# Pairs of weight blocks packed column by column in turns in a two-block transformer kernel

## The chip, the cores and the metric

The kernel runs on one core of a Trainium2 chip. The metric is the device time of one execution in microseconds. Before the change it is 1784.51 us, the median of three runs (1778.77, 1784.51 and 1785.51).

## What is computed

Two transformer blocks of different make run one after the other on 256 positions of width 1024, each with two layers. Everything is float32. Per layer the work is dominated by products of the activations with weight matrices that are used once:

```
h = rmsnorm(x, g);  proj = h @ w_in[l]            # first block: 1024 x 7168
merged = gate0*(.. @ w_ret_out) + gate1*(.. @ w_sc_out) + gate2*(.. @ w_cf_out)
x = x + rmsnorm(merged @ w_o[l], g)
up = causal_dwconv(rmsnorm(x, g) @ w_up[l])       # 1024 x 5632
x = x + rmsnorm((silu(gate) * val) @ w_down[l], g)
...
z = rms(x, g) @ w_in_2[l]                         # second block: three attention-like branches
x = x + merged @ w_out_2[l]
x = x + (silu(g) * u) @ w_down_2[l]
```

Between them stand retention, short and long depthwise convolutions, an mLSTM, a top-k sparse attention and a differential attention, all small beside the weight products.

## The kernel before

All weights are packed on the host into one stream of chunks of 128 partitions by 1024 columns of float32. A chunk holds eight **blocks** of 128 x 128 (`CB = 8`, line 26). `plan()` (line 66) lists the jobs in the order in which the kernel takes them; `pack_weights` (line 127) cuts each job's weights into blocks in the order in which they are used, and puts block i at columns 128 (i mod 8) of chunk i // 8.

On the chip, `Weights.load_to` (line 302) loads chunks by SyncE's queue into four buffers `wraw`. `Weights.ensure` (line 311) splits each chunk into two float32r tiles: ScalarE writes the rounded part `whi` (line 326), VectorE the remainder `wlo` (the subtraction at line 328, recorded at line 417). `Weights.take` (line 336) hands out the next n blocks of a chunk as slices of `whi` and `wlo`; four chunks, listed by `whole_chunks`, are handed out unsplit as `wraw`.

`Gen.job` (line 492) does one job. Kind "B" takes one block at a time: the block is the stationary operand (128 x 128), the moving operand is one 128 x 256 slice of the activations, also split (`hh` and `hl`, `yh` and `yl`, `fh` and `fl`). Three products per block add into one PSUM accumulator `acc`: hi x hi, hi x lo and lo x hi (lines 515 to 518); `self.mm` records all of them at line 405. For an unsplit block there is one float32 product, which the trace shows as four passes. Kind "A" (line 531; the values of the attention branches) takes four blocks at once and uses them as a moving operand of 512 columns, with the activations as the stationary one. At fixed points of a job, `self.side()` lets the other tasks issue their instructions, so now and then products of theirs (into `sp` tiles) stand between those of the jobs.

Before the change, a block that is a stationary operand is 128 columns in a row: 512 bytes in each partition, at a step of 4 bytes.

Of the kernel before, what the change touches and what calls it, by code (L numbers as in the profile page):

```python
# [17 lines left out]
P = 128  # L18
# [108 lines left out]
def pack_weights(inputs):  # L127
    blocks = []
    cache = {}
    for arr, idx, kind, nk, cols in plan():  # L130
        key = (arr, idx)
        if key not in cache:
            cache[key] = np.asarray(inputs[arr])[idx]
        w = cache[key]
        if kind == "B":
            c = np.concatenate(cols)
            t = w[:, np.maximum(c, 0)]
            if (c < 0).any():
                t = np.where(c[None, :] < 0, np.zeros_like(t), t)
            n = len(cols)  # L140
            blocks.append(t.reshape(nk, P, n, P).transpose(0, 2, 1, 3).reshape(nk * n, P, P))
        else:
            t = w[:, cols].reshape(nk, P, 4, P).transpose(0, 2, 1, 3).reshape(nk * 4, P, P)
            blocks.append(t)
    n = sum(b.shape[0] for b in blocks)
    tot = -(-n // CB) * CB
    out = np.zeros((tot // CB, P, CB, P), np.float32)
    i = 0
    for b in blocks:
        for j in range(b.shape[0]):  # L150
            out[(i + j) // CB, :, (i + j) % CB, :] = b[j]
        i += b.shape[0]
    return out.reshape(tot // CB, P, CW)
# [129 lines left out]
class Weights:  # L283
# [52 lines left out]
    def take(self, n=1):  # L336
        c, b = divmod(self.cur, CB)
        assert b + n <= CB
        self.cur += n
        s = slice(b * P, (b + n) * P)  # L340
        return [y[:, s] for y in self.parts[c]]

# [1294 lines left out]
```

## Time and profile before

| | |
|---|---|
| median of three runs | 1784.51 us |
| the profiled execution, its own time | 1783.79 us |
| its span, first to last instruction | 1782.1 us |
| TensorE products (PE) | busy 1770.8 us (99%), 14462 |
| TensorE weight loads (PEld) | busy 1723.9 us (97%), 14462 |
| VectorE (DVE) | busy 1360.8 us (76%) |
| ScalarE (ACT) | busy 1110.6 us (62%) |
| GpSimd (POOL) | busy 69.7 us (4%) |
| read from HBM | 312.80 MB, 176 GB/s over the span |

PE and PEld are two rows of the same engine: a product (MATMUL) and the load of its stationary operand (LDWEIGHTS). Both are pipelined: each row lasts longer than the time from its start to the next one's start, so busy shares say little, and the rate is read from starts. The chain of waits follows the work back from the last instruction and merges neighbours on one engine and tile into pieces: a piece gives its start, its length and its number of instructions. [...]

### The profile page before, as it was taken

The page shows a single profiled execution, that of the slowest core. Times are in us where ns is not written, and L with a number is a line of the kernel's source. Part 1 is how long each engine was busy: PE and PEld are TensorE (multiplying, and loading weights), DVE is VectorE, ACT ScalarE, POOL GpSimd, SP SyncE. Part 2 cuts the span into 40 slices and gives each one's busy share as a digit, 9 for nine tenths or more (in the row PEclk, how much of TensorE's full clock was granted, in tenths as well). Part 3 has the DMA queues.
Part 4 walks back from the last instruction along what each step waited for, and adds up shares of the span by engine and source line. Part 5 has one row for each costly group of instructions (what it writes and reads, how often), then busy time and mean ns, then how long its engine had stood idle before and what let it go on. Part 6 is the DMA issues. An engine that isn't in the chain of part 4 may idle for free.

```text
span 1782.1 us, 35765 instructions
## 1 busy us (share of the span) xinstructions
PE 1770.8 (99%) x14462; PEld 1723.9 (97%) x14462; DVE 1360.8 (76%) x2082; ACT 1110.6 (62%) x1787; POOL 69.7 (4%) x144
## 2 busy tenths in 40 slices
PE   8999999999999999999999999999999999999999
PEld 8999999999999999999998999999999999999999
DVE  8998689866999779883988877855569887687553
ACT  7676568755666568764676666644457666655442
POOL 0000000000000000000022100000001210000000
PEclk9999999999999999999999999999999999999999
DMA  7655545555555545555555644555555664455553
GB/s 269 195 177 187 191 143 202 190 189 172 200 177 190 180 149 195 190 189 166 164 191 181 210 133 146 190 185 187 188 185 172 202 196 137 144 188 189 188 189 121
DMA packets 94648, 322.52 MB, mean 181 GB/s; under 512 B 12257, under 2 KB 16913, under 8 KB 94482
## 3 DMA queue, kind: packets, MB, share of 16 engines
q1 hardware_dynamic: 91010, 314.15, 53.1%
q0 software_dynamic: 3328, 6.09, 1.2%
q8 instruction: 113, 1.85, 0.4%
q14 instruction: 53, 0.43, 0.1%
q10 hardware_dynamic: 144, 0.00, 0.0%
HBM read 312.80 MB, written 1.10 MB: 176 GB/s over the span
## 4 chain that ended last, share of the span: by engine, by line
PE 97%; DVE 1%; DMA 1%; issue 1%; ACT 0%; POOL 0%; SPq 0%; DVEq 0%; ACTq 0%; POOLq 0%
PE acc L405 90%; PE sp L405 6%; PE sp L410 1%; DMA Wm<-rows 0%; DMA tmp<-dq 0%; DMA x<-x 0%; DVE sc L1169 0%; DVE x L417 0%; DVE m L1168 0%; DVE yw L422 0%; DVE wlo L417 0%; ACT sd L447 0%; DVE dq L417 0%; ACT whi L326 0%; DVE Wm L428 0%
## 5 line engine op out<-in xcount | busy, mean ns | idle before, releaser
L326 ACT ACTIVATE whi<-wraw 128x1024 fp32r<-128x1024 f32 (+1 forms) x575 | 606.5, 1057 | 529.6 <-PE acc L405 359.6
L417 DVE TENSOR_TENSOR wlo<-wraw,whi 128x1024 fp32r<-128x1024 f32 (+1 forms) x575 | 697.0, 1218 | 285.9 <-ACT whi L326 284.8
L405 PE MATMUL acc<-hh,whi 128*128 128x256 f32 x2832 | 791.4, 280 | 0.0
L405 PE MATMUL acc<-hl,whi 128*128 128x256 f32 x2832 | 791.0, 280 | 0.0
L405 PE MATMUL acc<-hh,wlo 128*128 128x256 f32 x2832 | 789.8, 280 | 0.0
L405 PEld LDWEIGHTS acc<-hh,whi 128*128 128x128 f32 x2832 | 534.0, 189 | 5.5 <-issue 3.7
L405 PEld LDWEIGHTS acc<-hh,wlo 128*128 128x128 f32 x2832 | 534.4, 189 | 1.1 <-issue 0.8
L405 PEld LDWEIGHTS acc<-hl,whi 128*128 128x128 f32 x2832 | 532.0, 188 | 1.9 <-issue 1.2
L405 PE MATMUL acc<-yh,whi 128*128 128x256 f32 x1280 | 268.5, 283 | 6.1 <-ACT whi L326 6.1
L405 PE MATMUL acc<-yh,wlo 128*128 128x256 f32 x832 | 230.8, 282 | 0.0
L405 PEld LDWEIGHTS acc<-yh,whi 128*128 128x128 f32 x1280 | 210.4, 190 | 6.9 <-ACT whi L326 6.1
L405 PE MATMUL acc<-fh,wlo 128*128 128x256 f32 x704 | 197.9, 281 | 0.0
L405 PE MATMUL acc<-fl,whi 128*128 128x256 f32 x704 | 197.7, 281 | 0.0
L405 PE MATMUL acc<-fh,whi 128*128 128x256 f32 x704 | 197.5, 281 | 0.0
L405 PEld LDWEIGHTS acc<-yh,wlo 128*128 128x128 f32 x832 | 156.7, 190 | 0.4
L405 PEld LDWEIGHTS acc<-fh,wlo 128*128 128x128 f32 x704 | 133.6, 190 | 0.0
L405 PEld LDWEIGHTS acc<-fh,whi 128*128 128x128 f32 x704 | 133.5, 190 | 0.0
L405 PEld LDWEIGHTS acc<-fl,whi 128*128 128x128 f32 x704 | 132.2, 188 | 0.0
L405 PE MATMUL acc<-yl,whi 128*128 128x256 f32 x384 | 107.5, 281 | 0.0
L405 PEld LDWEIGHTS acc<-yl,whi 128*128 128x128 f32 x384 | 72.2, 188 | 0.2
L447 ACT ACT_TABLE_LOAD x50 | 64.2, 1283 | 5.3 <-DVE Wm L428 2.8
L422 DVE SCALAR_TENSOR_TENSOR up<-z,prm,up 128x254 f32<-128x254 f32 (+1 forms) x128 | 55.1, 476 | 0.0
(282 smaller groups left out, 1812.1 us busy)
## 6 DMA issues: line engine op xcount, KB each, us to landing
wraw<-stream SPq DMA_DIRECT2D x581, 512.0 KB, 3.4
kr<-rows SPq DMA_DIRECT2D x32, 64.0 KB, 3.1
dec<-decay SPq DMA_DIRECT2D x2, 768.0 KB, 4.2
x<-x SPq DMA_DIRECT2D x4, 256.0 KB, 6.2
rf<-rows SPq DMA_DIRECT2D x8, 128.0 KB, 3.6
tmp<-dq POOLq DMA_DIRECT2D x16, 64.0 KB, 2.9
Wm<-rows SPq DMA_DIRECT2D x8, 128.0 KB, 3.2
tmp<-dk POOLq DMA_DIRECT2D x16, 64.0 KB, 4.0
```

Of the source, the lines that this page charges most:

```text
L326: nc.scalar.activation(h[:, s], r[:, s], AF.Copy)
L405: return self.nc.tensor.matmul(out, lhsT, rhs, start=start, stop=stop, **kw)
L410: return self.nc.tensor.transpose(out, in_, self.c("ident")[:k, :k])
L417: self.recent = self.nc.vector.tensor_tensor(out=out, in0=a, in1=b, op=op)
L422: return self.nc.vector.scalar_tensor_tensor(out, a, s, b, op0=op0, op1=op1)
L447: return self.nc.scalar.activation(out, in_, f, **kw)
```

## The change

On the host, the blocks of a kind "B" job are taken in pairs (2j, 2j + 1), and the 256 columns of a pair are laid out in turns: column 0 of the first block, column 0 of the second, column 1 of the first, and so on. In the kernel, `take` with n = 1 no longer returns 128 columns in a row but every second column of the pair's 256, from offset 0 for the even block and 1 for the odd one: the step is 8 bytes. Kind "A" jobs are packed and taken as before. The loads of the chunks and the two instructions that split them see the same shapes and sizes.

```
--- before.py
+++ after.py
@@ -138,7 +138,9 @@
             if (c < 0).any():
                 t = np.where(c[None, :] < 0, np.zeros_like(t), t)
             n = len(cols)
-            blocks.append(t.reshape(nk, P, n, P).transpose(0, 2, 1, 3).reshape(nk * n, P, P))
+
+            t = t.reshape(nk, P, n, P).transpose(0, 2, 1, 3).reshape(nk * n // 2, 2, P, P)
+            blocks.append(t.transpose(0, 2, 3, 1).reshape(-1, P, 2, P).transpose(0, 2, 1, 3).reshape(-1, P, P))
         else:
             t = w[:, cols].reshape(nk, P, 4, P).transpose(0, 2, 1, 3).reshape(nk * 4, P, P)
             blocks.append(t)
@@ -337,6 +339,10 @@
         c, b = divmod(self.cur, CB)
         assert b + n <= CB
         self.cur += n
+        if n == 1:
+
+            s = slice((b & ~1) * P, (b | 1) * P + P)
+            return [y[:, s].rearrange("p (c h) -> p h c", h=2)[:, b & 1] for y in self.parts[c]]
         s = slice(b * P, (b + n) * P)
         return [y[:, s] for y in self.parts[c]]
```

Compiled, both programs issue the same instructions in the same order on every engine; only the access pattern of the stationary operands differs. The packing on the host is not part of the metric.

## Rows read from the trace of the kernel before

**Rows 1.** The profile's page: busy times, the granted clock, and the chain's shares.
```profile
PE 1770.8 (99%) x14462; PEld 1723.9 (97%) x14462; DVE 1360.8 (76%) x2082; ACT 1110.6 (62%) x1787; POOL 69.7 (4%) x144
...
PEclk9999999999999999999999999999999999999999
...
PE acc L405 90%; PE sp L405 6%; PE sp L410 1%; DMA Wm<-rows 0%; DMA tmp<-dq 0%; DMA x<-x 0%; DVE sc L1169 0%; DVE x L417 0%; DVE m L1168 0%; DVE yw L422 0%; DVE wlo L417 0%; ACT sd L447 0%; DVE dq L417 0%; ACT whi L326 0%; DVE Wm L428 0%
```

**Rows 2.** Chain of waits, its six long pieces: start us, length us, what, count.
```profile
165.13 66.31 PE acc L405 x563
...
246.80 177.61 PE acc L405 x1508
...
593.51 58.06 PE acc L405 x493
...
667.05 177.61 PE acc L405 x1508
...
1135.80 173.37 PE acc L405 x1472
...
1599.29 179.15 PE acc L405 x1521
```

**Rows 3.** Chain of waits, pieces of windows at 1567 to 1590 and 1096 to 1126 us.
```profile
1566.90 23.12 PE acc L405 x204
...
1095.92 30.15 PE acc L405 x266
```

**Rows 4.** Groups of products (page, --by-form): line, engine, tiles, shapes, count | busy us, mean ns.
```profile
L405 PE MATMUL acc<-hh,whi 128*128 128x256 f32 x2832 | 791.4, 280 | 0.0
...
L405 PE MATMUL acc<-yh,whi 128*128 128x256 f32 x1280 | 268.5, 283 | 6.1 <-ACT whi L326 6.1
...
L405 PE MATMUL acc<-yh,wlo 128*128 128x256 f32 x832 | 230.8, 282 | 0.0
...
L405 PE MATMUL acc<-fh,whi 128*128 128x256 f32 x704 | 197.5, 281 | 0.0
...
L405 PE MATMUL acc<-yl,whi 128*128 128x256 f32 x384 | 107.5, 281 | 0.0
```

**Rows 5.** Chain pieces within two kind "A" jobs (512-column products), windows at 44 and 465 us.
```profile
44.43 4.35 PE acc L405 x19
...
464.85 4.90 PE acc L405 x21
```

**Rows 6.** Timeline of PE, then of PEld, at 365 us: start us, length us, instruction.
```profile
365.00 0.28 PE L405 MATMUL acc<-fl,whi 128*128 128x256 f32 x1
365.12 0.28 PE L405 MATMUL acc<-fh,wlo 128*128 128x256 f32 x1
...
365.01 0.19 PEld L405 LDWEIGHTS acc<-fh,wlo 128*128 128x128 f32 x1
365.12 0.19 PEld L405 LDWEIGHTS acc<-fh,whi 128*128 128x128 f32 x1
```

**Rows 7.** Groups of weight loads of 128 and of 8 columns: count | busy us, mean ns.
```profile
L405 PEld LDWEIGHTS acc<-hh,wlo 128*128 128x128 f32 x2832 | 534.4, 189 | 1.1 <-issue 0.8
...
L405 PEld LDWEIGHTS sp<-sqt,cst 128*8 128x8 f32 x32 | 2.4, 89 | 3.5 <-ACT sv L447 0.4
```

**Rows 8.** Unsplit float32 blocks: six passes in the PE timeline, and their group.
```profile
239.78 1.46 PE L405 MATMUL acc<-yw,wraw 128*128 128x256 f32 x6
...
L405 PE MATMUL acc<-yw,wraw 128*128 128x256 f32 x128 | 28.7, 382 | 1.0 <-DVE yw L422 1.0
```

**Rows 9.** Busy time by window: window, us, PE PEld DVE ACT POOL, PEclk, DMA share, GB/s.
```profile
247.00:424.00 177.00, 177.00 (x1505) 177.00 (x1504) 135.76 (x211) 120.26 (x203) 0.00 (x0) 1.00 0.56 188
```

**Rows 10.** The two groups that split the chunks, from the page.
```profile
L326 ACT ACTIVATE whi<-wraw 128x1024 fp32r<-128x1024 f32 (+1 forms) x575 | 606.5, 1057 | 529.6 <-PE acc L405 359.6
L417 DVE TENSOR_TENSOR wlo<-wraw,whi 128x1024 fp32r<-128x1024 f32 (+1 forms) x575 | 697.0, 1218 | 285.9 <-ACT whi L326 284.8
```

More of the change, by code (lines that the diff above doesn't have):

```diff
@@ L140, in pack_weights @@
             n = len(cols)
-            blocks.append(t.reshape(nk, P, n, P).transpose(0, 2, 1, 3).reshape(nk * n, P, P))
+            t = t.reshape(nk, P, n, P).transpose(0, 2, 1, 3).reshape(nk * n // 2, 2, P, P)
+            blocks.append(t.transpose(0, 2, 3, 1).reshape(-1, P, 2, P).transpose(0, 2, 1, 3).reshape(-1, P, P))
         else:
@@ L339, in take @@
         self.cur += n
+        if n == 1:
+            s = slice((b & ~1) * P, (b | 1) * P + P)
+            return [y[:, s].rearrange("p (c h) -> p h c", h=2)[:, b & 1] for y in self.parts[c]]
         s = slice(b * P, (b + n) * P)
```

## The prediction

> **What bounds the kernel now.** I read the page first. TensorE's products are busy 99% of the span, and by the chain of waits 97% of the time is TensorE's, 90% of it at line 405 in `acc` tiles [rows 1]: nothing but the weight products sets the end. [...]
>
> Busy shares do not tell how fast the products follow each other, so I went to the pieces of the chain next, where length by count gives the time per product. The six long pieces give 66.31/563, 177.61/1508, 58.06/493, 177.61/1508, 173.37/1472 and 179.15/1521 us, each 117.8 ns; together 832.1 us and 7065 products [rows 2]. But that is not the only rate. In other stretches the pieces give 23.12/204 = 113.3 ns and 30.15/266 = 113.3 ns [rows 3]. Instruction, shape and partly even the tiles are the same. A stream of products runs at one of the two rates for hundreds of products; it is usually another task's product between them that moves it to the other. I call them the **high** rate (117.78 ns) and the **low** one (113.33 ns).
>
> How many products are concerned: 3 x 2832 of `hh` and `hl`, 1280 + 832 + 384 of `yh` and `yl`, 3 x 704 of `fh` and `fl`, together 13104 [rows 4] (pairs of rows that differ in hi and lo alone have the same count). So 7065 of them stand in the long high pieces and 6039 elsewhere.
>
> Where do the 4.45 ns between the rates come from? The "A" jobs tell. Their products stream 512 columns instead of 256, but load the same 128. Near 44 us, with low-rate products around them, they take 4.35/19 = 228.9 ns each, near 465 us, in a high stretch, 4.90/21 = 233.3 ns [rows 5]. The difference is again 4.4 ns, not twice that: it goes with the load, not with the columns that stream. And the load does run under the stream: each LDWEIGHTS starts within 0.01 us of a product, and lasts 0.19 us while the next starts 0.12 us later [rows 6]. My reading is that the high rate is a standing collision of each load with the stream under which it runs, fixed by their phase, and the low rate is the same stream without it. No row shows the collision itself.
>
> **The change part by part.** No instruction is added, removed or moved, and no bytes are added to any transfer. What changes is the step of the stationary operand in the 13104 split products, from 4 to 8 bytes, and with it how the loads fall among the reads of the stream.
>
> *Loads at step 8.* No row has a stationary operand with a step, so the cost is bounded. A load of 128 columns lasts 189 ns, one of 8 columns 89 ns [rows 7]: (189 - 89)/120 = 0.83 ns per column, 106.7 ns for 128. That lies just inside the 113.3 ns of a product, and the next load cannot start before the next product does [rows 6]: whatever a step adds to a load shows in full in the rate.
> Lower end: the stream alone. Passes of float32, at half the column rate, take (1.46 - 0.38)/5 = 216 ns for 256 columns [rows 8] (0.38 is the mean length of one); half of that is 108 ns, and the load's own 106.7 ns are about the same. Below 108 ns nothing in the trace leads.
> Upper end: every column costs two column times, 213 ns per load.
> The value I take is that the collision goes and all products run at the low rate, 113.33 ns. It is the nearest row: the same instruction at the same columns, seen in the same execution. With a step of 8 bytes the load moves through memory at 8 bytes in 0.83 ns, the stream at 4 bytes in 0.42 ns or so, thus at the same pace, which makes a lasting phase without collisions plausible, not more.
>
> The sum: in the long pieces 7065 x (117.78 - 113.33) = 31.4 us. Of the 6039 others some already run at the low rate [rows 3]; if all ran at the high one they would give 6039 x 4.45 = 26.9 us, if none, 0. I take about a quarter, 6 us, because the pieces at the low rate are the long ones there. The profiled execution took 1783.8 us: 1783.8 - 31.4 - 6 = **1746 us**, within 1725 to 1752 by the two bounds, and 1757 if a few stretches stay high. The median of the runs is 1784.5, 0.7 us above the profiled one, which I neglect.
>
> *What else is touched, at zero.* The unsplit blocks are also taken with a step: 128 passes at 216 ns [rows 8], under which even a load of 213 ns finds room. The "A" jobs keep their operands. The chunks' splits are the same; VectorE needs 1.22 us per chunk and ScalarE 1.06 [rows 10], and a chunk feeds 24 products, 24 x 113.33 = 2.72 us instead of 2.83. In a long high stretch VectorE is busy 135.76 of 177 us and the DMA engines 0.56 of the time [rows 9]; the same work in 177 x 113.33/117.78 = 170.3 us makes 80% and 0.58. So the cover holds: nothing else is late next at the low rate. At 108 ns, VectorE's 1360.8 us [rows 1] would be 81% of the span, so some mixing stretches might give part of it back.
>
> **The rivals.**
> *No effect (R0).* The loads take as long at step 8 as at 4, and the phases fall as before, since the order of the instructions is the same: 1784 us. For it: one column per 0.83 ns is slow enough that the memory may not care which column. Against it: the rate already depends on phase, so the loads do care about something. [...]
>
> *More collisions (R1), slower.* Its place is the load in the product's loop: in 8-byte steps it touches twice the memory in the same time, and meets the stream in either phase. It decides as soon as a load is lengthened at all. If every product pays the present price once, the long pieces stay and the other 6039, now at about 113.33 + 4.45/4 = 114.4 ns on average, go to 117.78: +20 us, 1804 us. If each pays it twice: 1746 + 13104 x 8.9 ns = 1863 us. For it: the price exists and goes with the load [rows 5].
>
> *Half-rate loads (R2), slower by far.* If each column at a step costs two column times, the loop of load and product grows by 106.7 ns: 1746 + 13104 x 106.7 ns = about 3140 us. For it: the load fills 106.7 of 113.3 ns already [rows 7]. Against it: a column takes 0.83 ns now, twice the 0.42 ns in which a moving column is read. [...] No row here shows a load with a step.
>
> *All overhead goes (R3).* The low rate itself holds 5.3 ns over the stream's 108. If a step frees that too: 7065 x 9.8 + 6039 x 6.4 ns = 69 + 39 = 108 us less, 1676 us. Against it: no stretch of split products in the trace runs below 113.3 ns.
>
> **How the numbers follow.** Forecast 0.44, R0 0.22, R1 0.16, R2 0.08, R3 0.10. About 0.5%, 9 us, is what a measurement here can tell from no change. Faster by more than that: forecast and R3, 0.54; within: R0, 0.22; slower: R1 and R2, 0.24. The range from 1675 to 1806 us holds the forecast, R3, R0 and the cheaper half of R1 (0.08), together 0.84; R2 and the dearer half of R1 lie outside. The forecast's own range is 1725 to 1757.
>
> **What would show each step right or wrong.** In the chain after the change, the pieces of 1508 products should last 1508 x 113.33 ns = 170.9 us instead of 177.6; at 177.6 it is R0, at 184 or more R1, near 163 R3. The "A" products should take 229 ns in both places. LDWEIGHTS of `hh,wlo` should stay near 189 ns; near 290 ns it is R2. VectorE and ScalarE should be busy as long as before, 1361 and 1111 us, in a shorter span; if their idle time before PE shrinks to nothing, the gain ends there. The forecast is wrong if pieces at two rates still stand side by side, or if a rate appears that the trace before does not have.

## The result, and the profile after

The change makes the kernel slower: 1832.85 us, the median of four runs (1832.16 to 1834.33), against 1782.06 us of four runs before (1778.77 to 1785.51). The ratio is 1.0286, 95% interval 1.0261 to 1.0311. The profiled execution after took 1832.16 us with a span of 1830.4 us, 48.3 us more than the span before.

Two facts on the unsplit float32 blocks in the part on the kernel before need mending: each shows in the trace as two passes, not four, and eight chunks, not four, are handed out unsplit (8 chunks x 8 blocks x 2 passes = the 128 passes of [rows 8]). No number of the prediction changes.

The page after, in the lines that answer to [rows 1], [rows 7] and [rows 10]; the groups give count | busy us, mean ns | idle time before them:
```profile
PE 1818.6 (99%) x14462; PEld 1773.2 (97%) x14462; DVE 1364.7 (75%) x2082; ACT 1111.6 (61%) x1787; POOL 68.3 (4%) x144
...
PEclk9999999999999999999999999999999999999999
...
L411 PEld LDWEIGHTS acc<-hh,wlo 128*128 128x128 f32 x2832 | 549.6, 194 | 1.1 <-issue 0.8
...
L328 ACT ACTIVATE whi<-wraw 128x1024 fp32r<-128x1024 f32 (+1 forms) x575 | 607.5, 1058 | 579.1 <-PE acc L411 397.2
L423 DVE TENSOR_TENSOR wlo<-wraw,whi 128x1024 fp32r<-128x1024 f32 (+1 forms) x575 | 698.4, 1218 | 316.1 <-ACT whi L328 314.5
```
ScalarE and VectorE are as busy as before. ScalarE's group waits 50 us longer, mostly for TensorE, and VectorE's group 30 us longer, for ScalarE. The granted clock is 1.00 of the full one on the mean, before and after. A load's row is 5 ns longer than in [rows 7]. So the time went into the rate of the products, and the chain of waits shows it: first the six pieces of [rows 2], then one of the shorter ones. The columns are start us, length us, what, count.
```profile
171.45 67.56 PE acc L411 x563
...
254.55 180.96 PE acc L411 x1508
...
611.04 59.16 PE acc L411 x493
...
685.73 180.96 PE acc L411 x1508
...
1167.32 176.64 PE acc L411 x1472
...
1644.30 182.53 PE acc L411 x1521
...
1587.19 54.61 PE acc L411 x455
```
The shorter piece in the kernel before:
```profile
1545.23 51.59 PE acc L405 x455
```
Each of the six is now 120.0 ns per product (180.96/1508) instead of 117.78. The piece of 455 goes from 113.4 to 120.0 ns. In uninterrupted stretches there is one rate left, **120.0 ns**, and it is neither the high nor the low one of before.

The account has two terms. The six pieces sum to 847.8 us, 832.1 before: +15.7 us for 7065 products, 2.22 ns each. If the other 6039 products pay all of the rest, 48.3 - 15.7 = 32.6 us, that is 5.4 ns each, and their mean before was 114.6 ns: most of them had run at the low rate. The starts in the two traces bear this out, since both have the same products in the same order: from one product to the next the split products outside the six pieces take 32.6 us more, and all products that are not split ones together 0.3 us less. The prediction's "about a quarter" for these 6039, 114.4 ns on average, was thus about right.

The "A" jobs, which the change does not touch, stayed: 21 products take 4.81 us, 229 ns each, as near 44 us before [rows 5]. In the second such job, which had stood in a high stretch, 18 take 4.12 us, also 229 ns. The unsplit passes now load at a step too, and kept their (4.26 - 0.38)/18 = 216 ns [rows 8]. The two rows are a piece of the chain, and one of the PE timeline:
```profile
45.31 4.81 PE acc L411 x21
```
```profile
244.77 4.26 PE L411 MATMUL acc<-yw,wraw 128*128 128x256 f32 x19
```

### The profile page after: what moved, and what is told of

Same layout as the page of the kernel before. It is cut to its first block, busy times and chain, and to the rows that moved or that the text cites. A ratio compares the mean times of both kernels' runs of the same rounds, so it can differ in the third digit from the quotient of the medians.

```text
span 1830.4 us, 35765 instructions
## 1 busy us (share of the span) xinstructions
PE 1818.6 (99%) x14462; PEld 1773.2 (97%) x14462; DVE 1364.7 (75%) x2082; ACT 1111.6 (61%) x1787; POOL 68.3 (4%) x144
## 4 chain that ended last, share of the span: by engine, by line
PE 97%; DVE 1%; DMA 0%; ACT 0%; issue 0%; SPq 0%; DVEq 0%
PE acc L411 91%; PE sp L411 6%; PE sp L416 1%; DMA Wm<-rows 0%; DMA x<-x 0%; DVE wlo L423 0%; DVE sc L1175 0%; ACT L453 0%; DVE x L423 0%; DVE m L1174 0%; DVE yw L428 0%; ACT sd L453 0%; DVE dq L423 0%; ACT whi L328 0%; DVE Wm L428 0%
## 5 line engine op out<-in xcount | busy, mean ns | idle before, releaser
L411 PE MATMUL acc<-hl,whi 128*128 128x256 f32 x2832 | 800.4, 283 | 0.0
L411 PE MATMUL acc<-hh,whi 128*128 128x256 f32 x2832 | 799.7, 283 | 0.0
L411 PEld LDWEIGHTS acc<-hh,whi 128*128 128x128 f32 x2832 | 549.4, 194 | 5.5 <-issue 3.7
L411 PEld LDWEIGHTS acc<-hl,whi 128*128 128x128 f32 x2832 | 549.1, 194 | 1.9 <-issue 1.2
L411 PEld LDWEIGHTS acc<-hh,wlo 128*128 128x128 f32 x2832 | 549.6, 194 | 1.1 <-issue 0.8
L411 PE MATMUL acc<-yh,whi 128*128 128x256 f32 x1280 | 274.1, 286 | 6.4 <-ACT whi L328 6.4
L411 PEld LDWEIGHTS acc<-yh,whi 128*128 128x128 f32 x1280 | 215.8, 195 | 7.2 <-ACT whi L328 6.4
L411 PEld LDWEIGHTS acc<-yh,wlo 128*128 128x128 f32 x832 | 160.8, 195 | 0.3
L411 PEld LDWEIGHTS acc<-fl,whi 128*128 128x128 f32 x704 | 136.3, 194 | 0.0
```

Of the source, the lines that this page charges most:

```text
L411: return self.nc.tensor.matmul(out, lhsT, rhs, start=start, stop=stop, **kw)
```

## The experiments

Rates below are length by count of a piece. In the stream kernels a piece holds a start of up to 0.1 us, so 96 products at 113.3 ns show as 113.4 to 114.1. In the short streams of the first run it is the other way round: the first and last starts of the loads, 201.3 and 206.6 us at step 4, 207.1 and 212.7 at step 8, give 113 and 119 ns, each within 2, so the 110.4 and 116.5 of the pieces may be a little low.

### Streams on an idle core

A kernel of its own that keeps none of the transformer: like products in streams, with stationary operands at several steps (a cut):
```
for name, step in (("four", 1), ("eight", 2), ("twelve", 3), ("sixteen", 4), ("thirtytwo", 8)):
    stream(name, N, lambda j: cols(v, j, step, P), mov)
...
for name, step in (("shortfour", 1), ("shorteight", 2), ("shortsixteen", 4)):
    stream(name, 24, lambda j: cols(wr, j, step, P), lambda j: xr[:, 64 * (j % 4):64 * (j % 4) + 64])
```


> This kernel leaves out the whole computation (its output is its input x) and only runs streams of products on an otherwise idle core, 96 per stream (48 of 512 columns, 24 float32 ones), with the step of the stationary operand varied. Theory A: a load is longer by what it covers in memory, whatever runs beside it: 113.3 ns per product at a step of 4 bytes, 120.0 at 8, 126.7 at 12, 133.3 at 16, more at 32; with float32 products of 64 columns (which wait for loads) about 112 at 4, 119 at 8, 132 at 16. Theory B: the price is a collision with the stream under which the load runs: 113.3 or 117.8 at 4, 120 at every larger step, and the short float32 products stay at 112 at every step. Theory C: any step over 4 bytes costs a load the same surcharge: 120 at 8, 12, 16 and 32, and the short products go to 119 at 8 and 16. Stationary operands of 64 columns (loads half as long): A and C 108 to 110 at every step, since the load is then no longer the bound; B more at a step than without. Streams in the kernel's own order of operands after six different lead-ins: under all theories 120.0 at a step of 8; at 4 bytes some at 113.3 and some at 117.8, if it is the phase at the start that picks the rate.

The chain's pieces (names give the step in bytes; "half" has 64 stationary columns; "wide" has 512 moving ones; "short" streams are float32 products of 64 columns, two passes each, short enough for the load to set the rate: by the 216 ns of [rows 8] 64 columns stream in 54 ns, an estimate):
```profile
33.25 11.51 PE four L40 x96
...
45.19 11.51 PE eight L40 x96
...
57.13 16.80 PE twelve L40 x96
...
74.36 22.30 PE sixteen L40 x96
...
97.10 23.01 PE thirtytwo L40 x96
...
132.08 10.90 PE halffour L40 x96
...
166.85 10.91 PE widefour L40 x48
...
201.64 5.30 PE shortfour L40 x48
...
207.43 5.59 PE shorteight L40 x48
...
213.51 11.09 PE shortsixteen L40 x48
```
None of the three theories holds at steps 12 and 16. Three things follow.

First, load alone (the short streams): 110.4 ns at step 4, 116.5 at 8, 231.0 at 16. The long stream at step 16 takes as long as the load alone, 232.3 ns, and the one at step 12 stands between, at 175.0. From step 8 to 16 the time goes with the memory that 128 columns cover in a partition: 116.5 ns for 1024 bytes, 175.0 for 1536 and 232.3 for 2048 are all 0.113 to 0.114 ns per byte. At step 32 it hardly grows further, to 239.7 ns for 4096 bytes.

Second, at these places step 4 is no better than step 8: both 119.9 ns. Streams in the kernel's own order of products give 119.8 to 121.1 ns after six different leads at either step, except for the first at step 4, 129.9 ns, whose longest load row is 337 ns where the other five have 192; the two rates expected at step 4 did not come. So the step alone was not the whole story, and what the kernel has at step 4 that this stream lacks had to be found.

Third, 64 columns at step 4 run at 113.5 ns under 256 moving columns, though they load half as many columns: no stream of 256 moving columns in this study runs below 113.3, and the 108 ns that the prediction's lower end took from float32 passes do not show here.

### Step 16 in the kernel
Four blocks in turns instead of two (a cut, against the changed kernel):
```
-            s = slice((b & ~1) * P, (b | 1) * P + P)
-            return [y[:, s].rearrange("p (c h) -> p h c", h=2)[:, b & 1] for y in self.parts[c]]
+            s = slice(b // 4 * 4 * P, (b // 4 + 1) * 4 * P)
+            return [y[:, s].rearrange("p (c h) -> p h c", h=4)[:, b % 4] for y in self.parts[c]]
```


> Four blocks in turns instead of two, so a step of 16 bytes. Theory A (a load pays for what it covers): 133.3 ns per product, 1833 + 13104 x 13.3 ns = about 2007 us. Theories B and C (a price that does not grow with the step): 120.0 ns, about 1833 us. If a column per 16 bytes needs two column times: 220 ns per product, over 3100 us.

3337.47 us, against 1785.62 before. A long piece of the chain:
```profile
453.55 355.11 PE acc L423 x1508
```
That is 235.5 ns per product; the second piece of 1508 takes 351.77 us, 233.3 ns each. Theories A to C fall here too, and the fourth expectation, two column times, comes near. The price of the rival of half-rate loads (R2) is real, but sets in between steps 8 and 16: 120.0 ns at 8, on the idle core 175.0 at 12.

### Only the rounded part at step 8
`whi` stays in turns; VectorE writes `wlo` in rows, so two of three products have a step (a cut):
```
+            p = self.parts[c]
+            hi = p[0][:, s].rearrange("p (c h) -> p h c", h=2)[:, b & 1]
+            return [hi] + [y[:, b * P:(b + 1) * P] for y in p[1:]]
```


> Only the rounded parts (whi) have a step of 8 bytes; VectorE writes the remainders (wlo) back as blocks in a row, so one load of three is as before the change. Theory A and C (the price belongs to each load): (2 x 120.0 + 113.3)/3 = 117.8 ns per product, about 1833 - 13104 x 2.2 ns = 1804 us. Theory B (the price is a matter of the phase of the whole stream): one of the rates 113.3, 117.8 or 120.0 for long stretches, so 1746 to 1833 us, and at 120.0 as likely as at another.

1819.18 us, between the expected 1804 and 1833. The groups of loads, then a piece of the chain:
```profile
L431 PEld LDWEIGHTS acc<-hh,whi 128*128 128x128 f32 x2832 | 558.5, 197 | 5.5 <-issue 3.7
...
L431 PEld LDWEIGHTS acc<-hh,wlo 128*128 128x128 f32 x2832 | 533.4, 189 | 1.1 <-issue 0.8
```
```profile
253.22 179.33 PE acc L431 x1508
```
118.9 ns per product: strided loads last 8 ns longer (197 ns) than those in rows (189), which are as before [rows 7], and the mixture settles at a rate of its own, which neither theory had. The cost is no fixed price per strided load: two of three loads bring half of the 2.22 ns in this piece and, counted from the low rate, 5.6 of the 6.7 ns.

### The place of the weights
Streams again, in the kernel's order of split products, at 14 distances between the stationary and the moving tile within a partition, at steps 4 and 8 (a cut):
```
def lhs(j):
    b, o = j // 3 % 8, off // 4 + 4096 * (j % 3 == 2)
    ...
```


> This kernel leaves out the whole computation (its output is its input x). Streams of 96 split products in the kernel's own order of operands on an otherwise idle core; the place of the stationary tile relative to the moving one is varied (0, 8, 16, 32, 48, 64, 96, 128, 160, 192, 256, 320, 384 and 448 bytes), at a step of 4 and of 8 bytes, each after two lead-ins. In the first stream kernel both lay at the same place modulo 512 bytes and a step of 4 gave 120.0 ns, while 8 bytes to the side gave 115.6; in the full kernel they lie 64 bytes apart modulo 128. Theory A (a load is longer by itself at a step of 8): at 8 bytes 117.5 to 120 ns at every place and after each lead-in, at 4 bytes 113.3 to 120 depending on the place. Theory B (only the collision costs): at 8 bytes the rate depends on the place as well, and some place gives 113.3; at 4 bytes 113.3, 117.8 or 120.0, the same for places 128 bytes apart.

Pieces (four/eight: step in bytes; distances a = 0, b = 8, c = 16, e = 48, f = 64, h = 128 bytes; p: one float32 product of 256 columns ahead, q: a short one after it):
```profile
33.08 11.51 PE fourap L41 x96
...
57.18 11.14 PE fourbp L41 x96
...
152.01 10.89 PE fourfp L41 x96
...
198.50 11.51 PE fourhp L41 x96
...
413.24 11.39 PE eightcp L41 x96
...
473.63 11.72 PE eighteq L41 x96
```
At step 4 the place alone moves the rate from 113.4 (64 bytes; 113.6 at 320) over 116.0 (8) to 119.9 (0 and 128). At step 8 all 28 streams lie between the last two rows, 118.6 and 122.1; the place with 113.3 that theory B expected is not among them. In the compiled kernel `whi` and `wlo` start at 128 and all the split activations at 64 modulo 256 bytes, so the weights stand 64 bytes from the activations modulo 256: the one distance tried, with its repeat at 320, that gives the low rate.

### The kernels at another place
Before and after, each with the pad ahead of the activations cut by 64 bytes, which puts the weights at distance 128:
```
-        self.xpool.tile([P, 32], F32, name="xpad")
+        self.xpool.tile([P, 16], F32, name="xpad")
```


> The kernel before, with the activations 64 bytes lower, so that weights and activations lie 128 bytes apart modulo 256 instead of 64. If the place decides at a step of 4, as in the stream kernel (120.0 ns at 128, 113.3 at 64): 120.0 ns per product, 1784 + 13104 x 3.7 ns = about 1833 us, with one rate throughout, the time of the changed kernel without its step. If the place does not matter in the full kernel: 1784 us, with the two rates as before.

> The changed kernel with the same 64 bytes. Theory A (at a step of 8 the load itself is the bound, wherever it lies): 120.0 ns as before the move, 1833 us within 4. Theory B (a collision that depends on the place): another rate, more than 10 us off.

Before moved takes 1824.78 us (1778.89 for the kernel before on the same chip), after moved 1838.97. Two long pieces of the chain of the first, then one of the second:
```profile
254.89 178.95 PE acc L405 x1508
...
683.47 180.96 PE acc L405 x1508
```
```profile
255.67 180.96 PE acc L411 x1508
```
Before moved has two rates again, 118.7 and 120.0 ns, not the one expected: two of its six long pieces run at the first, four at the second. After moved keeps 120.0 ns in five of the six and has 121.1 in the last (184.22/1521). This is the sharpest result of the study: the kernel before, with no step at all, loses 45.9 us when the distance changes, nearly what the change costs, while the changed kernel loses 6 us, more than theory A's 4 and less than theory B's 10. Each of the two moved kernels ran once; the runs of the kernel before spread over 7 us.

### What picks the high or the low rate
Streams at step 4, at the kernel's distance of 64 and six near it, begun at each of the three products of a block, after different interruptions.


> This kernel leaves out the whole computation. Streams of 96 split products at a step of 4 bytes, at the place of the full kernel (64 bytes modulo 256) after six lead-ins and starting with each of the three products of a block, and at places 40, 56, 60, 68, 72 and 80 after two lead-ins. If the start picks the rate, some streams at 64 keep 117.8 ns and others 113.3; if the place alone does, all at 64 have 113.3 and the high rate of the full kernel comes from elsewhere. A place at which every stream has 113.3 would bring the full kernel to about 1746 us.

Pieces at distance 64 (x, y: first or second product of a block; q a short float32 product ahead, r a transpose, p one float32 product of 256 columns):
```profile
33.94 10.91 PE kindaxp L43 x96
...
45.45 10.96 PE kindaxq L43 x96
...
56.94 11.31 PE kindaxr L43 x96
...
104.65 11.31 PE kindayp L43 x96
```
113.6, 114.2, 117.8 and 117.8 ns. The same stream at the same place keeps one of two rates, and what ran just before it picks which: always the high one (117.8) after a transpose, always the low one (113.3 to 114.7) after a short product and after the three other leads, and after one float32 product it depends on the start (113.6 or 117.8). At the six other distances no stream ran at the low rate (117.9 to 120.1 ns). So [rows 2] and [rows 3] are two lasting phases of one stream, as the prediction read them.

### A short product ahead of the long stretches
If that is right, the kernel before can be put into the low phase. Six dummy products (float32, 64 columns, into an accumulator that the next product clears) are placed behind the last product of a job: one in each layer of the first block's mixer and one in each of the four feed-forward parts (a cut).
```
+            if kick:
+                with self.tc.issue_after(self.done_mm.ins):
+                    self.mm(accs[0][:, :64], self.ones[:, :P], self.ones[:, :64])
...
-                    self.job(evac, mov)
+                    self.job(evac, mov, kick=i == 4)
```


> The kernel before (step 4), with six float32 products of 64 columns put in front of jobs: one in each of the two first-block mixers, and one at the third or fourth job of each of the four feed-forward parts. In the stream kernel such a product always left the stream at 113.3 ns. If the long high pieces are only a phase that the last interruption picked: about 6900 products at 113.33 instead of 117.78 ns, -30.7 us, plus 6 x 0.3 us: about 1753 us, and the pieces of 1508 products at 113.3 ns. If the high rate comes from something else in those stretches (their tiles, other engines): 1782 to 1786 us.

The same with eighteen, to see whether the added ones change a phase or only cost their time. The twelve more are one ahead of each output projection and each down projection (`kick=i == 0`) and a second one in each feed-forward part (a cut, against the kernel with six):
```
-                    self.job(evac, mov, kick=i == 4)
+                    self.job(evac, mov, kick=i in (4, 12))
```


> The same with eighteen such products: also in front of the output projections, of the down projections and of the twelfth feed-forward job. If the low rate, once reached, holds without interruption, the added ones gain nothing and cost 12 x 0.3 us: about 1756 us. If it is lost on the way (at the change from one moving tile to the next, say), they bring it back, and this one is the faster of the two.

With six: 1759.79 us (1759.0 to 1760.64), ratio to the kernel before 0.9866, interval 0.9851 to 0.988. With eighteen: 1762.42 us, ratio 0.9879 (0.9863 to 0.9896). Pieces of the chain with six: first a whole stretch that was aimed at and, from the windows 246 to 258 and 260 to 416 us, its parts ahead of and behind the short product, which stands between them; then two stretches that were not aimed at. Last a piece with eighteen:
```profile
245.31 171.68 PE acc L405 x1510
...
245.90 12.13 PE acc L405 x103
...
259.90 156.17 PE acc L405 x1378
...
586.24 58.06 PE acc L405 x493
...
1080.08 42.04 PE acc L405 x356
```
```profile
244.86 172.18 PE acc L405 x1514
```
Within one stretch the rate falls from 117.8 ns (12.13/103) ahead of the short product to 113.3 behind it (156.17/1378), and stays there to the end. The stretch of 493 without one stays high, and the one of 356 went from 113.9 ns to 118.1, picked by another interruption; these two (2.2 and 1.5 us) are a good part of the 7 us by which the time exceeds the expected 1753. Two thirds of the gain that the prediction expected from the step (24 of 37 us) thus exist, and are to be had without a step. This is the version that beats both kernels. With eighteen the time is 2.6 us longer than with six: an added product brings the stretch of 493 down too (57.46 us for 495, 116.1 ns), but most of the others fall into stretches that are already low, and only cost their time. In these stretches the low phase holds once it is entered.

### Loads by themselves
Products of 16 columns, short enough to leave only loads (a cut):
```
stream("load" + name, 24, lambda j: cols(wr, j, step, n), lambda j: xr[:, 64 * (j % 4):64 * (j % 4) + 16], n)
```


> This kernel leaves out the whole computation. Float32 products of 16 columns, whose rate is that of their loads, on an otherwise idle core. A load of 128 columns at steps of 4, 8, 12, 16, 20, 24 and 32 bytes; of 96 columns at 4, 8 and 16; of 112 at 8; of 64 at 16. [...] If a step merely adds a fixed 5.6 ns up to 8 bytes: 96 columns at 8 bytes 91, 112 columns 104, 64 columns at 16 the same as 64 at 4.

The page's row of the clock, then two pieces of the chain (128 columns at steps 8 and 16):
```profile
PEclk9999999999555555555555555555555555555555
...
40.17 10.05 PE loadb L40 x48
...
62.36 10.97 PE loadd L40 x48
```
The expected numbers were for the full clock, and the granted clock fell to 0.5 near the end of the first of these streams: the row has 9 tenths or more up to 38.4 us, in slices of 3.84 us, and 5 from there on; the stream ends at 39.1 us. At that clock steps 8 and 12 take 209 ns each, and step 16 takes 228.5, about as much as the long stream at step 16 in the first run, 232.3, where the mean clock was 0.986. So the price at step 16 hardly goes with the granted clock. At steps 20 and 24 it takes 216.3 and 217.9 ns, less than at 16, though it covers more memory. For the question of the kernel the run decides nothing.

### Shorter loads and longer streams
The last question: at step 8 a load alone takes 116.5 ns, more than the stream's 113.3. Is it simply the longer of the two (a cut)?
```
for i, n in enumerate((128, 120, 112, 96, 80, 64, 32)):
    stream("cols" + word + "abcdefg"[i], N, split(step, 64, n), act(256), n)
...
for i, width in enumerate((272, 288, 320, 384, 512)):
    stream("wide" + word + "abcde"[i], 60, split(step, 64, P), act(width))
```


> Leaves out the transformer blocks: streams of like products on an idle core, the stationary tile 64 bytes from the moving one (modulo 256), after a short float32 product as lead. Stationaries of 128, 120, 112, 96, 80, 64 and 32 columns at steps of 4 and 8 bytes under 256 moving columns; then 128 columns under 272, 288, 320, 384 and 512 moving columns. Theory L (the load at step 8 lasts about 117.5 ns and is the bound, nothing else): at step 8 the rate falls to 113.3 ns as soon as the load is shorter than the stream, thus at 112 columns and fewer, and under 288 or more moving columns both steps give 0.4427 ns per column (127.5, 141.7, 170, 226.7). Theory C (each load in 8-byte steps also takes time from the stream under which it runs, whether it is hidden or not): at step 8 the rate stays above 113.3 at every number of columns, falling slowly, some 119 ns at 112, 117 to 118 at 64; and under 288 to 512 moving columns step 8 stays 6 to 9 ns above step 4. Step 4: 113.3 for all numbers of columns by both.

Pieces (letters as in the lists above):
```profile
33.51 10.95 PE colsfoura L40 x96
...
57.06 11.55 PE colsfourc L40 x96
...
104.88 10.90 PE colsfourg L40 x96
...
153.61 14.05 PE widefoure L40 x60
...
206.90 11.47 PE colseightc L40 x96
...
255.00 11.17 PE colseightg L40 x96
...
304.44 13.86 PE wideeighte L40 x60
```
Theory L, that the load's length is the bound and nothing else, falls. With 112 columns the load is shorter than the stream (116.5 x 112/128 = 102 ns, an estimate), and step 8 still runs at 119.5 ns; even 32 columns do not reach the limit (116.4). For the kernel's 128 columns both remain: a load of 116.5 ns alone is too long for the low rate, and a price beside it is paid by shorter loads too. No run tells how much of the 120.0 ns is which. Theory C holds under 256 moving columns, but not in its other parts: step 4 is at the limit with 128 and 32 columns only (114.1 and 113.5) and at 120.3 with 112; and under 512 moving columns step 4 is the slower one, 234.2 against 231.0, while under 384 it is the faster, 174.3 against 178.0. So nearly every pair of load and stream tried here pays some nanoseconds, at either step. **What the kernel before had in its low stretches was an exception**: 128 columns in rows, 64 bytes from the activations, in a phase that costs nothing. At step 8 no stream of this study found such a phase; the start within a block was not varied there.

## Why the prediction was wrong

It said 1746 us, within 1675 to 1806, and "faster" at 0.54. The kernel went to 1833, outside the range on the other side.

- *What bounds the kernel*: right. TensorE's products set the end before and after, and the other engines only wait longer.
- *Two rates as phases of one stream*: right. The streams after different interruptions showed that the last interruption picks the rate, and six short products turned it into 24 us less.
- *A price that goes with the load, not with the columns that stream*: right for the two rates of the kernel before [rows 5], but not in general. On the idle core at distance 0, 256 columns pay 6.6 ns over 113.3, while 512 columns pay next to nothing (227.3 ns against 2 x 113.3).
- *"The value I take is that the collision goes and all products run at the low rate"*: this is the step that failed. It rested on "at the same pace, which makes a lasting phase without collisions plausible". Shown is the reverse: 28 streams of 128 columns at 14 distances had no such phase at step 8, and in the kernel all six long pieces run at 120.0 ns. The nearest row misled: that row, the low rate, is a property of one distance and one phase, and the change destroys the phase. Instead of 13104 products at 113.33 ns there are 13104 at 120.0, a difference of 13104 x 6.67 ns = 87 us, which is the 1833 - 1746 by which the forecast missed.
- *The lower end, 108 ns, and R3*: wrong. Half the time of a float32 pass is not the split stream's limit; with 64 and with 32 columns to load, 113.5 ns were left.
- *Load alone, 106.7 ns at step 4*: about right; 110.4 was measured. What a step adds to it the prediction put at nothing, though it said that whatever a step adds shows in full in the rate. At step 8 the load alone takes 116.5 ns (float32 loads), 6.1 more, so that it no longer fits under the stream's 113.3: this by itself rules out the low rate, and shorter loads show that it is not the whole price (119.5 ns with 112 columns).
- *R1, more collisions*: the right direction and, as far as the runs go, the right reading, "meets the stream in either phase" and "as soon as a load is lengthened at all", at a chance of 0.16. The collision itself no run shows. Its sizes were whole prices of 4.45 ns over the low rate, once (1804) or twice (1863); measured are 6.67 ns, one and a half. The range ended at 1806 because "once" left the long pieces where they were; they too rose by 2.22 ns.
- *R0*: wrong, 120.0 ns came where 117.78 had stood. What the prediction held against it, that "the loads do care about something", holds beyond the phase: on an otherwise idle core, the same products took 113.4 or 119.9 ns by the distance of the two operands alone.
- *R2*: no such cost at step 8, where the `hh,wlo` load's row lasts 194 ns and not 290; at step 16 it came, 3337 us.
- *The cover*: VectorE, ScalarE and the DMA queues have more time than before, and the 1378 products at 113.3 ns in the version with six short products show that they also keep up at the low rate.
- *The signs named*: "if a rate appears that the trace before does not have" is what came; 180.96 us for 1508 products lies between the marks of R0 (177.6) and of R1 (184 or more).

What stays open is on what load and stream collide, if that is what they do, and how much of the 120.0 ns is the longer load. At step 4 the rates at distances 64 and 320 bytes are alike (113.4 and 113.6 ns), as are those at 0, 128 and 256 (119.9); no run shows the part of the memory at which they meet, nor why 120.0 ns is so common.

## What to carry to other kernels

When one instruction shows two rates in one trace, find what picks the rate before changing an operand: compare streams by the relative place of the operands and by the instruction just ahead of them. A layout that looks neutral can rest on such an exception, so any change of address, step or size near a saturated TensorE has to be measured, and a few nanoseconds per product are worth bounding in both directions. Here a product of 64 columns at the right six places was worth 1.3%, and 64 bytes of padding 2.6%.

## What the runs showed of the hardware

- From step 8 to 16 the time of a load goes with the memory that it covers: 116.5, 175.0 and 232.3 ns for 128 columns at steps 8, 12 and 16, 0.113 to 0.114 ns per byte; at step 32 it is 239.7 ns, and at half the granted clock 216.3 and 217.9 at steps 20 and 24. The price at step 16 is about the same at half the granted clock, 228.5 ns.
- The rate of 256-column float32r products at step 4 depended on the distance between the stationary and the moving operand: at best 113.4 ns at 64 bytes, 119.9 at 0 and 128.
- A stream kept its phase for over a thousand products (117.8 ns for 1508 in the kernel before), and one short product in it settled which: 117.8 ns ahead of it, 113.3 for the 1378 products behind it.
- After sixty products of 256 columns, and towards the end of a first stream of 16-column products, the granted clock went from full to 0.5 at about 38.4 us and stayed there to the end, 153.7 us, through eleven more such streams, with one float32 product between each two.
